# RMS norm sums by VectorE 32x32 turns and a folding matmul in place of TensorE transposes

## The chip, the cores and the metric

One core of a Trainium2 chip runs the whole program. The metric is the device time of one execution in microseconds (us), as the median of several runs. The engines are TensorE (PE, with its weight loads listed apart as PEld), VectorE (DVE), ScalarE (ACT), GpSimd (POOL) and SyncE (SP, which issues most DMAs). Each takes its own instructions in order.

## The reference

The kernel computes one encoder layer for two sequences (prompt and sample, each 512 tokens of width 1024) in fp32. What the change touches are its norms:

```
def rms_norm(x, g):
    xf = x.astype(jnp.float32)
    y = xf * lax.rsqrt(jnp.mean(xf * xf, axis=-1, keepdims=True) + EPS)
    return (y * g.astype(jnp.float32)).astype(x.dtype)
...
    x = x + 0.5 * swiglu(rms_norm(x, ffn1_norm), ffn1_w_gate, ffn1_w_up, ffn1_w_down)
    h = rms_norm(x, mix_norm)
    proj = h @ w_in
...
    att = gqa_block_attention(aq, ak, av)
    mem = mlstm_bidirectional(mq, mk, mv, gate_pre, mlstm_gate_bias, o_pre, mlstm_head_norm)
    merged = jax.nn.sigmoid(g_att) * (att @ w_up_att) + jax.nn.sigmoid(g_mlstm) * (mem @ w_up_mlstm)
    x = x + merged @ w_out
    x = x + 0.5 * swiglu(rms_norm(x, ffn2_norm), ffn2_w_gate, ffn2_w_up, ffn2_w_down)
```

Inside the memory (`mlstm_bidirectional`, four heads of width 128) each head's output has a norm of its own:

```
    h = h * lax.rsqrt(jnp.mean(h * h, axis=-1, keepdims=True) + EPS)
    h = h.reshape(B, S, M_WIDTH) * head_norm.astype(jnp.float32)
    return (jax.nn.sigmoid(o_pre.astype(jnp.float32)) * h).astype(q.dtype)
```

## The kernel before, in words

Activations lie turned: the 128 partitions hold channels, the free axis holds the 512 tokens, so x is eight tiles of 128x512. A norm's mean over channels is then a sum over partitions (and over the eight tiles). Every large product is split into a high and a low part, and three matmuls with 512 columns replace one.

The program runs FFN1 for both sequences, its down projection (`ffn_down`), the mixing stage (`mix`, a generator: `m0` for the prompt, `m1` for the sample), and FFN2 with its end. A scheduler orders the instructions by a running priority; `shifted(n)` moves a stretch's priority later by n. In the attention the PE order is pinned: scores (L1039), gate projections (L776), key transposes (L1055) and values (L1066) stand in program order, and `among` puts a few gate matmuls between them.

A norm goes like this. ACT squares the tiles and an accumulator of 128x512 collects them (`sq_add`, L148 to L156). `col_sums` (L199) transposes the accumulator on PE in four 128x128 pieces (L202), and DVE reduces each piece (L204) to a column: 128x4, one number per token. `rstd_cols` (L158) forms the reciprocal root by an integer guess and three Newton steps on 128x4 (L161 to L191). `bcast_psum` (L208) spreads it again by four PE transposes of broadcast columns (L212), and for x `bcast_cols` copies the result from PSUM into an SBUF tile R (L218). The norms of x stand at four places:

- A: x of m0 at the end of FFN1's down projection (`mid_stats`, L1578);
- B: x of m1, inside the attention of m0 (`mid_parts(1)`, called as `extra` at L1125 after head 2 or 3);
- D: x of m0 before FFN2, inside the attention of m1 (`parts2(0)`);
- F: x of m1 at the start of FFN2 (`stats2(1)`).

The attention part of `mix` scales its projections by R and by the columns r. In the memory part `mem_head` builds a head's weights and `mem_out` (L1218) its output in a PSUM tile: squares (ACT L1238), gates (DVE L1240), norms: `col_sums`, `rstd_cols`, and, with priority moved 160 later, the spread, DVE's scaling of the gated head by its gain and the spread root (L1244, into a row of the tile `box`), and the residual split into `mem` (L1245). While the heads run, PE fills in with matmuls of the attention's merge and of later gates. Behind head 3 come eight gate projections `mem_gate` (L1156): 24 matmuls each into a PSUM tile "mm", which DVE empties into a t2 tile (L1159, times R). Of "mm" banks there are three, of "pst" and "pss" two each, of "pso" one; of the SBUF tiles t2 eleven.

Of the kernel before, what the change touches and what calls it, by code (L numbers as in the profile page):

```python
# [26 lines left out]
def encoder(ctx, tc, I, outs):  # L27
# [44 lines left out]
    def tables(shapes):  # L72

        t = spool.tile([P, 7 * S // 2], F32, tag="tab", bufs=1, name=nm("tab"))
        out, c = [], 0
        for sh in shapes:
            n = sh[0] * (sh[1] if len(sh) > 1 else 1)
            v = t[:, c:c + n]
            out.append(v if len(sh) == 1 else v.rearrange("p (a b) -> p a b", b=sh[1]))
            c += n  # L80
        return out
# [76 lines left out]
    def rstd_cols(v, width, n):  # L158

        a = spool.tile([P, width], F32, tag=f"rs{width}", bufs=5 if width > 2 else 10, name=nm("rs"))  # L160
        nc.vector.tensor_scalar(a, v, 1.0 / n, EPS, op0=ALU.mult, op1=ALU.add)  # L161
        return rsqrt_cols(a, width)
# [29 lines left out]
            y = r  # L192
        return y

    def stats(acc):

        return rstd_cols(col_sums(acc), 4, D)

    def col_sums(acc, bs=(0, 1, 2, 3)):  # L199
        p = PT()  # L200
        for b in bs:
            nc.tensor.transpose(p[:, b * P:(b + 1) * P], acc[:, b * P:(b + 1) * P], ident)  # L202
        c = spool.tile([P, len(bs)], F32, tag=f"cs{len(bs)}", bufs=4, name=nm("cs"))
        nc.vector.tensor_reduce(c, p[:, bs[0] * P:(bs[-1] + 1) * P].rearrange("p (b d) -> p b d", d=P), axis=AX.X,  # L204
                                op=ALU.add)
        return c

    def bcast_psum(r):  # L208

        pr = PT()  # L210
        for b in range(4):
            nc.tensor.transpose(pr[:, b * P:(b + 1) * P], r[:, b:b + 1].to_broadcast([P, P]), ident)  # L212
        return pr

    def bcast_cols(r):
        pr = bcast_psum(r)
        R = T2(F32, "R")
        nc.vector.tensor_copy(R, pr)  # L218
        return R

    def fetch_w(view, behind=None):
# [475 lines left out]

    def mix_consts():
        pin = tc.keep_in_program_order
        tri, msk, *cgs = tables(((4, P), (2, P)) + ((4, DA),) * 4)  # L700
        pin(nc.gpsimd.dma_start(tri, I["c_tri"]))
        pin(nc.gpsimd.dma_start(msk, I["c_mask"]))
        rope = T2(F32, "f2").rearrange("p (c b d) -> p c b d", c=2, b=4)
        pin(nc.gpsimd.dma_start(rope, I["c_rope"].rearrange("c (b p) d -> p c b d", p=P)))
        for name, sc in (("q_norm", DA ** -0.5), ("k_norm", 1.0)):
            gb = cpool.tile([P, DA], F32, name=nm("gb"))
            pin(nc.gpsimd.dma_start(gb, I[name].partition_broadcast(P).rearrange("p a d -> p (a d)")))
            if sc != 1.0:
                G_.tensor_scalar(gb, gb, sc, None, op0=ALU.mult)
            cg, sg = cgs.pop(0), cgs.pop(0)  # L710
            G_.tensor_tensor(cg, rope[:, 0], gb.unsqueeze(1).to_broadcast([P, 4, DA]), op=ALU.mult)
            sgv = sg.rearrange("p b (i two) -> p b i two", two=2)
            srv = rope[:, 1].rearrange("p b (i two) -> p b i two", two=2)
            gbv = gb.rearrange("p (i two) -> p i two", two=2)
            for e in range(2):
                G_.tensor_tensor(sgv[:, :, :, e], srv[:, :, :, e],
                                 gbv[:, :, 1 - e].unsqueeze(1).to_broadcast([P, 4, DA // 2]), op=ALU.mult)
            tabs.append((cg, sg))
        tabs.extend((tri, msk))
# [76 lines left out]
    def mix(s, xh, xl, early=None, extra=None, after=None):  # L796
# [100 lines left out]
        def gates():  # L897
            Gb = Gt.rearrange("p (b c) -> p b c", b=4)
            V_.tensor_tensor(Gb, Gb, gbias.unsqueeze(1).to_broadcast([P, 4, 16]), op=ALU.add)
            Gv = Gt.rearrange("p (b d g h) -> p b d g h", b=4, d=2, g=2)  # L900

            Fs, Fv = gs("Fs")
            Is, Iv = gs("Is")
            for dst, g in ((Fv, 1), (Iv, 0)):
                G_.tensor_copy(dst[:, 0], Gv[:, :, 0, g, :])
                for b in range(4):
                    G_.tensor_copy(dst[:, 1, 3 - b], Gv[:, b, 1, g, :])
            fa, _ = gs("fa")
            V_.scalar_tensor_tensor(fa, Fs, -1.0, Fs, op0=ALU.mult, op1=ALU.min)
            nc.scalar.activation(fa, fa, AF.Exp)  # L910
            nc.scalar.activation(fa, fa, AF.Ln, bias=1.0)
            nc.scalar.activation(warm, fa[:, 0:1], AF.Exp)
            Lt, _ = gs("Lt")
            V_.scalar_tensor_tensor(Lt, Fs, 0.0, fa, op0=ALU.min, op1=ALU.subtract)
            p = PT()
            for d in range(2):
                rhs = Lt[:, d * 16:(d + 1) * 16]
                for j, lhs in enumerate((tabs[2][:, 2 * d, :], tabs[2][:, 2 * d + 1, :], ones)):
                    nc.tensor.matmul(p[:, j * 32 + d * 16:j * 32 + (d + 1) * 16], lhs, rhs, start=True, stop=True)
            V_.tensor_copy(cs, p[:, 0:96])  # L920
            et, ev = gs("et")
            V_.tensor_tensor(et, Is, cs[:, 32:64], op=ALU.add)
            p = PT()
            nc.tensor.transpose(p[0:32, 0:P], et, ident)
            rows = F2()[0:32]
            er, run = rows[:, 0:P], rows[:, P:2 * P]
            V_.tensor_copy(er, p[0:32, 0:P])
            nc.sync.dma_start(ebuf.rearrange("d b h s -> (d b h) s"), er)
            V_.tensor_tensor_scan(run[:, ::-1], er[:, ::-1], er[:, ::-1], NEG, op0=ALU.max, op1=ALU.max)
            V_.tensor_tensor_scan(run[0:16], er[0:16], er[0:16], NEG, op0=ALU.max, op1=ALU.max)  # L930
            top = rows[:, 2 * P:2 * P + 1]
            V_.tensor_reduce(top, er, axis=AX.X, op=ALU.max)
            return run, top
# [241 lines left out]
        def mem_head(h):  # L1175
# [39 lines left out]
                    V_.tensor_scalar(tf[:, up_], tb[:, up_], rb, None, op0=ALU.mult)  # L1215
            return Ts

        def mem_out(h, Ts):  # L1218
            vm = Vm[0]
            po = PO()  # L1220
            hs_ = slice(h * P, (h + 1) * P)
            turned = []
            for j in range(4 + 1):
                if j < 4:
                    p = PT()
                    for i in range(4):
                        nc.tensor.transpose(p[:, i * P:(i + 1) * P], Ts[i][0][:, j * P:(j + 1) * P], ident)
                    ph, pl = T2(F32R), T2(F32R)
                    split(p, ph, pl)
                    turned.append((j, ph, pl))  # L1230
                if j >= 1:
                    t, ph, pl = turned.pop(0)
                    with shifted(15):
                        for n, (a, b) in enumerate(((0, ph), (1, ph), (0, pl))):
                            nc.tensor.matmul(po, vm[:, a, t, hs_], b, start=(t == 0 and n == 0),  # L1235
                                             stop=(t == 3 and n == 2))
            h2 = T2()
            nc.scalar.activation(h2, po, AF.Square)  # L1238
            og = ogs[h]
            V_.scalar_tensor_tensor(og, og, 1.0, po, op0=ALU.add, op1=ALU.mult)  # L1240
            rh = rstd_cols(col_sums(h2), 4, DM)
            with shifted(160):
                Rh = bcast_psum(rh)
                V_.scalar_tensor_tensor(og, og, hn[:, h:h + 1], Rh, op0=ALU.mult, op1=ALU.mult)  # L1244
                split(og, mem[:, h, 0, :], mem[:, h, 1, :])  # L1245

        for h in range(HM):
            Ts = mem_head(h)
            if h == 0:
                go(*mem_values())  # L1250
            queue.append(merge_att(2 * h))
            fill(1)
            mem_out(h, Ts)
            if h + 2 < HM:
                queue.extend([out_gate(h + 2), mem_qk(h + 2, 0), mem_qk(h + 2, 1)])
            queue.append(merge_att(2 * h + 1))
            fill(99)

        mh, ml = A([P, KD, S], F32R, "mh"), A([P, KD, S], F32R, "ml")
# [317 lines left out]

    def mid_stats(s, a=0, b=0):  # L1578
        with shifted(a):
            r[s] = stats(accs[s])  # L1580
        with shifted(b):
            R[s] = bcast_cols(r[s])

    r = [None, None]
    R = [None, None]
# [11 lines left out]
    box()  # L1597

    def mid_parts(s):
        def one():  # L1600
            r[s] = stats(accs[s])

        def two():
            R[s] = bcast_cols(r[s])
        return one, two

    m0 = mix(0, *nhl[0], None, mid_parts(1), prep1)
# [12 lines left out]
        put(xc[B11 if d < HK_ else B21], d % HK_, xt)  # L1620

    def stats2(s):
        r[s] = stats(acc2[s])
        R2[s] = bcast_cols(r[s])

    def parts2(s):
        def one():
            r[s] = stats(acc2[s])

        def two():  # L1630
            R2[s] = bcast_cols(r[s])
        return one, two

    R2 = [None, None]
# [153 lines left out]
```

## Time and profile before

| | |
|---|---|
| time, median of 3 runs | 2062.38 us (2060.41 to 2063.18) |
| profiled execution, span from first to last instruction | 2059.1 us |
| median over that span | 3.3 us |
| granted TensorE clock in it | 0.999 |
| L202 in it (sums) | 52 transposes of 128x128, 32 for heads, 20 for x |
| L212 in it (spreads) | 52 transposes of 128x128, 48 of Newton results |
| L204, reduction of a transposed sum | 13, mean 688 ns |
| narrow Newton operation 128x4 (L188, L189, L191) | 36 each, mean 160 or 161 ns |

A span is shorter than the time of a run, which also holds what lies around the first and the last instruction. In the profile's rows stand the start, the duration, the engine, the line, the operation, output<-input, and in brackets how long the engine stood idle before and which engine's work ended that.

### The profile page before, as it was taken

To read this page: it belongs to the slowest core of one execution; us is meant where nothing else is said; L and a number is where in the kernel's file an instruction comes from. 1 tells how busy PE (TensorE), PEld (TensorE's weight loads), DVE (VectorE), ACT (ScalarE), POOL (GpSimd) and SP (SyncE) were. 2 spreads that over 40 slices of the span, in tenths; PEclk is the share of its full clock that TensorE was granted. 3 is DMA by queue.
4 is the path that set the end of the run, shared out by engine and by line. 5 is a ranking of instruction groups with operands and counts; after the bars stand their busy time and mean duration, and the time that the engine had idled before them with its cause. 6 is when DMAs were issued, how large, how long until landed. Compare 5 with 4: busy or idle time off the path is not lost.

```text
span 2059.1 us, 27038 instructions
## 1 busy us (share of the span) xinstructions
PE 2047.3 (99%) x9445; PEld 1691.3 (82%) x9445; DVE 1553.0 (75%) x2764; ACT 913.0 (44%) x1667; POOL 92.8 (5%) x108
## 2 busy tenths in 40 slices
PE   9999999999999999999999999999999999999998
PEld 7888888888888888888888888888888888888887
DVE  8888889886797787675566756455788888796797
ACT  7544444442235567563334553324544444443224
POOL 0000000001003000100120000001000000000001
PEclk9999999999999999999999999999999999999999
DMA  9656556799766753877684345677656555599753
GB/s 321 198 170 221 177 191 205 243 349 348 260 227 247 223 187 130 278 259 242 197 310 160 109 140 200 196 265 239 202 175 202 194 174 184 186 342 347 276 202 119
DMA packets 311015, 457.97 MB, mean 222 GB/s; under 512 B 20232, under 2 KB 182112, under 8 KB 309600
## 3 DMA queue, kind: packets, MB, share of 16 engines
q1 hardware_dynamic: 308800, 450.27, 64.6%
q0 software_dynamic: 1920, 5.72, 0.9%
q8 instruction: 74, 1.21, 0.2%
q14 instruction: 61, 0.50, 0.1%
q10 hardware_dynamic: 160, 0.27, 0.0%
HBM read 288.25 MB, written 167.94 MB: 222 GB/s over the span
## 4 chain that ended last, share of the span: by engine, by line
PE 97%; DVE 1%; ACT 1%; DMA 1%; issue 0%; SPq 0%; ACTq 0%; DVEq 0%
PE mm L789 15%; PE pso L332 12%; PE pst L332 12%; PE mm L332 10%; PE mm L590 8%; PE pss L332 6%; PE mm L776 6%; PE pst L590 4%; PE pss L590 4%; PE mm L756 4%; PE pso L590 3%; PE pso L1066 1%; PE pss L1039 1%; PE pst L1055 1%; PE pso L1235 1%; PE pss L1185 1%
## 5 line engine op out<-in xcount | busy, mean ns | idle before, releaser
L332 PE MATMUL pst<-xc,w 128*128 128x512 f32 x1056 | 253.6, 389 | 0.0
L332 PEld LDWEIGHTS pst<-xc,w 128*128 128x128 f32 x1056 | 198.3, 188 | 41.1
L332 PE MATMUL mm<-xc,w 128*128 128x512 f32 x972 | 229.9, 390 | 0.2 <-ACT f L340 0.2
L332 PEld LDWEIGHTS mm<-xc,w 128*128 128x128 f32 x972 | 181.9, 188 | 38.1 <-ACT f L340 0.6
L590 PE MATMUL mm<-rt,w 128*128 128x512 f32 x765 | 178.9, 389 | 0.0
L789 PE MATMUL mm<-xh,w 128*128 128x512 f32 x560 | 177.6, 393 | 0.0
L590 PEld LDWEIGHTS mm<-rt,w 128*128 128x128 f32 x765 | 143.6, 188 | 29.8
L290 ACT ACTIVATE w<-t 128x512 fp32r<-128x512 f32 x176 | 106.5, 627 | 135.7 <-issue 63.1
L291 DVE TENSOR_TENSOR w<-t,w 128x512 fp32r<-128x512 f32 x176 | 117.8, 688 | 47.9 <-ACT w L290 46.6
L332 PE MATMUL pss<-xc,w 128*128 128x512 f32 x528 | 126.8, 389 | 0.0
L332 PE MATMUL pso<-xc,w 128*128 128x512 f32 x528 | 126.8, 389 | 0.0
L332 PE MATMUL pso<-xc,f 128*128 128x512 f32 x528 | 126.8, 389 | 0.0
L789 PEld LDWEIGHTS mm<-xh,w 128*128 128x128 f32 x560 | 104.7, 188 | 21.2 <-DVE w L239 0.2
L332 PEld LDWEIGHTS pss<-xc,w 128*128 128x128 f32 x528 | 99.2, 188 | 20.5
L332 PEld LDWEIGHTS pso<-xc,w 128*128 128x128 f32 x528 | 99.1, 188 | 20.5
L332 PEld LDWEIGHTS pso<-xc,f 128*128 128x128 f32 x528 | 99.1, 188 | 20.5
L776 PE MATMUL mm<-xh,w 128*128 128x512 f32 x336 | 114.5, 401 | 0.0
L789 PE MATMUL mm<-xl,w 128*128 128x512 f32 x280 | 109.7, 392 | 0.0
L673 ACT ACTIVATE w<-wr 128x512 fp32r<-128x512 f32 x72 | 45.1, 632 | 137.0 <-PE pso L590 71.4
L673 ACT ACTIVATE w<-t 128x512 fp32r<-128x512 f32 x82 | 51.8, 632 | 107.4 <-PE pst L590 62.4
L590 PE MATMUL pst<-rt,w 128*128 128x512 f32 x396 | 93.7, 389 | 0.0
L590 PE MATMUL pss<-rt,w 128*128 128x512 f32 x396 | 93.7, 389 | 0.0
(407 smaller groups left out, 4037.5 us busy)
## 6 DMA issues: line engine op xcount, KB each, us to landing
rt<-rbuf SPq DMA_DIRECT2D x154, 512.0 KB, 5.7
wpark<-w SPq DMA_DIRECT2D x104, 512.0 KB, 3.4
w<-wpark SPq DMA_DIRECT2D x104, 512.0 KB, 4.8
wr<-in_ffn_w_gate_dram SPq DMA_DIRECT2D x62, 512.0 KB, 5.3
rbuf<-tab SPq DMA_DIRECT2D x102, 256.0 KB, 3.9
wr<-in_ffn_w_up_dram SPq DMA_DIRECT2D x44, 512.0 KB, 4.5
rbuf<-f SPq DMA_DIRECT2D x72, 256.0 KB, 4.1
wr<-in_w_in_dram SPq DMA_DIRECT2D x36, 512.0 KB, 5.7
```

Of the source, the lines that this page charges most:

```text
L290: pin(nc.scalar.activation(t[:, 0], src, AF.Copy))
L291: pin(V_.tensor_tensor(t[:, 1], src, f(t[:, 0]), op=ALU.subtract))
L332: nc.tensor.matmul(p, a[:, k, :], xt[:, b, k, :], start=(first and k == 0 and i == 0), stop=(k == HK_ - 1 and i == 2), skip_group_check=True)
L590: nc.tensor.matmul(p, u[:, a, d * P:(d + 1) * P], r[:, b, ts], start=(first and q == 0 and k == 0), stop=(q == len(us) - 1 and k == 2), sk ...
L673: nc.scalar.activation(hi, src, AF.Copy)
L756: nc.tensor.matmul(p[b][:, :N], a[:, k, bs], w_[:, kl, :], start=(k == 0 and i == 0), stop=(k == KD - 1 and i == 2))
L776: pin(nc.tensor.matmul(p[0], a[:, k, :], b, start=(k == 0 and i == 0), stop=(k == n - 1 and i == 2)))
L789: nc.tensor.matmul(p, a[:, k, :], b, start=(k == 0 and i == 0), stop=(k == n - 1 and i == 2))
L1039: pin(nc.tensor.matmul(p, qT[:, h, b * P:(b + 1) * P], kv[:, hk * 2 + j, :], start=(j == 0), stop=(j == 1)))
L1055: pin(nc.tensor.transpose(p[:, b * P:(b + 1) * P], Ps[b][:, kb * P:(kb + 1) * P], ident))
L1066: pin(nc.tensor.matmul(pos[h], Vst[:, kb, h // 4, :], w, start=(kb == 0 and i == 0), stop=(kb == 3 and i == 1)))
L1185: nc.tensor.matmul(p, qk[a][:, isl], qk[b], start=(n == 0), stop=(n == 2))
```

## The change

`col_sums` and `bcast_psum` are no longer used for the norms of x at mixing and FFN2 and for the heads. In their place:

- `block_sums`: DVE turns the 128x512 tile in blocks of 32x32 (STREAM_TRANSPOSE), so that a block's 32 channels lie along the free axis, and reduces them to 128x16. A partition then holds, for 16 tokens, the sum over 32 of the 128 channels.
- `block_rstd`: one matmul with the constant `fold`, which adds the four partitions that belong together and gives each the total; then the same Newton steps on 128x16 (or 128x64).
- `spread_rows`: a second DVE turn, of the root broadcast 32 times, gives the 128x512 tile that the PE transposes gave.
- `row_cols`: where the columns r are wanted too (A and B), four copies on POOL.
- For the heads, `mem_out` only leaves its 128x16 sums in `hsum`, a t2 tile that lives through the four heads. After head 3, `mem_norm` does the fold, the Newton steps and the spreads for all four at once, without the former shift of 160.

PE loses 96 transposes and gains six fold matmuls. `finish0` at the end of FFN2 and the start of the program keep their transposes.

```
+    def fold_const():
+        part_ = fold[:, 0:32]
+        for a in range(1, 4):
+            src = ident[:, 0:32] if a == 1 else part_
+            nc.gpsimd.tensor_tensor(part_, src, ident[:, a * 32:(a + 1) * 32], op=ALU.add)
+        nc.gpsimd.tensor_copy(fold[:, 32:P].rearrange("p (a j) -> p a j", j=32),
+                              part_.unsqueeze(1).to_broadcast([P, 3, 32]))
+
+    def block_sums(t, to):
+        q = T2()
+        nc.vector.transpose(q, t)
+        nc.vector.tensor_reduce(to, q.rearrange("p (n j) -> p n j", j=32), axis=AX.X, op=ALU.add)
+
+    def block_rstd(v, n, row):
...
+        p = PT()
+        nc.tensor.matmul(p[:, 0:w], fold, v, start=True, stop=True)
...
+        V.tensor_scalar(a, p[:, 0:w], 1.0 / n, EPS, op0=ALU.mult, op1=ALU.add)
...
+    def row_stats(acc):
+
+        row = T2()
+        block_sums(acc, row[:, 0:16])
+        return block_rstd(row[:, 0:16], D, row)
...
+    def row_cols(r16):
+
+        c = spool.tile([P, 4], F32, tag="rc4", bufs=2, name=nm("rc"))
+        for a in range(4):
+            ps_ = slice(a * 32, (a + 1) * 32)
+            nc.gpsimd.tensor_copy(c[ps_, :], r16[ps_, :].rearrange("p (b a) -> p a b", a=4)[:, a, :])
+        return c
+
+    def spread_rows(r16, R):
+
+        nc.vector.transpose(R.rearrange("p (n j) -> p n j", j=32), r16.unsqueeze(2).to_broadcast([P, 16, 32]))
         return R
...
+        hsum = T2()
+
         def mem_out(h, Ts):
...
-            rh = rstd_cols(col_sums(h2), 4, DM)
-            with shifted(160):
-                Rh = bcast_psum(rh)
+            block_sums(h2, hsum[:, h * 16:(h + 1) * 16])
+
+        def mem_norm():
+            rh = block_rstd(hsum[:, 0:64], DM, hsum)
+            for h in range(HM):
+                og = ogs[h]
+                Rh = spread_rows(rh[:, h * 16:(h + 1) * 16], T2())
                 V_.scalar_tensor_tensor(og, og, hn[:, h:h + 1], Rh, op0=ALU.mult, op1=ALU.mult)
                 split(og, mem[:, h, 0, :], mem[:, h, 1, :])
...
+            if h == HM - 1:
+                mem_norm()
             fill(99)
...
     def mid_parts(s):
+        got = []
+
         def one():
-            r[s] = stats(accs[s])
+            got.append(row_stats(accs[s]))
 
         def two():
-            R[s] = bcast_cols(r[s])
+            R[s] = spread_rows(got[0], T2(F32, "R"))
+            r[s] = row_cols(got[0])
         return one, two
```

`mid_stats`, `stats2` and `parts2` change in the same way (the last two without `row_cols`). Lines of the new kernel stand some 45 higher in the rows below: scores are L1084, the residual split is L718, the turn L223, its reduction L224, the fold L234, the spread L262, the evacuation of a memory gate L1204.

In the attention of m0 (place B), PE's rows before, from the values to the next score, a name and a number for each tile:

```order
L1066 MATMUL pso_6390<-t_603_6383,kv_5280 128x512
L1066 MATMUL pso_6390<-t_604_6384,kv_5280 128x512
L202 MATMUL pst_6432<-ident,R_5176 128x128 x4
L1039 MATMUL pss_6460<-kv_5280,qT_5283 128x512 x2
L776 MATMUL mm_6416<-xl_4890,w_6309 128x512
```

And in the changed kernel:

```order
L1111 MATMUL pso_6385<-t_595_6378,kv_5275 128x512
L1111 MATMUL pso_6385<-t_596_6379,kv_5275 128x512
L234 MATMUL pst_6431<-t_608_6427,fold 128x16
L1084 MATMUL pss_6445<-kv_5275,qT_5278 128x512 x2
L821 MATMUL mm_6411<-xl_4895,w_6304 128x512
```

The fold stands where the four transposes stood. The transposes read the accumulator R; the fold reads t_608, the row that DVE's reduction fills. DVE's rows before at that place:

```order
L1012 TENSOR_TENSOR box_5279<-box_5279,tab_4209 128x512
L239 TENSOR_TENSOR w_6410<-wr_6408,w_6410 128x1024
L1049 TENSOR_SCALAR t_608_6398<-t_608_6398,asm_6396 128x512
L674 TENSOR_TENSOR t_615_6424<-pst_6418,t_614_6423 128x512
L204 TENSOR_REDUCE cs_6437<-pst_6432 128x4
L1042 TENSOR_REDUCE asm_6463<-pss_6460 128x1
L161 TENSOR_SCALAR rs_6439<-cs_6437 128x4
```

And in the changed kernel:

```order
L1057 TENSOR_TENSOR box_5274<-box_5274,tab_4214 128x512
L283 TENSOR_TENSOR w_6405<-wr_6403,w_6405 128x1024
L1094 TENSOR_SCALAR t_600_6393<-t_600_6393,asm_6391 128x512
L718 TENSOR_TENSOR t_607_6419<-pst_6413,t_606_6418 128x512
L223 STREAM_TRANSPOSE t_609_6428<-R_5171 128x512
L1057 TENSOR_TENSOR box_5274<-box_5274,tab_4214 128x512
L224 TENSOR_REDUCE t_608_6427<-t_609_6428 128x16
L237 TENSOR_SCALAR t_608_6427<-pst_6431 128x16
```

The turn has the place behind the residual split that the reduction had; a box addition stands between it and its reduction, and the first Newton operation L237 reads the fold's PSUM tile.

At the end of m0's heads (place C), DVE's rows before, from the last residual split of the head's turned weights on: gate 0's evacuation (L1159) stands ahead of head 3's gating (L1240) and sums (L204).

```order
L674 TENSOR_TENSOR t_978_8120<-pst_8114,t_977_8119 128x512
L1159 TENSOR_TENSOR t_1003_8239<-mm_8214,R_5156 128x512
L1240 SCALAR_TENSOR_TENSOR box_5279<-box_5279,pso_8080 128x512
L204 TENSOR_REDUCE cs_8137<-pst_8132 128x4
L161 TENSOR_SCALAR rs_8139<-cs_8137 128x4
```

In the changed kernel, from the last Newton operation of `mem_norm` (L243) to the evacuations of gates 0 and 1 (mm_8102, mm_8138):

```order
L243 SCALAR_TENSOR_TENSOR t_755_7040<-t_755_7040 128x64
L262 STREAM_TRANSPOSE t_934_8036<-t_755_7040 128x512
L262 STREAM_TRANSPOSE t_935_8041<-t_755_7040 128x512
L1295 SCALAR_TENSOR_TENSOR box_5274<-box_5274,hn,t_934_8036 128x512
L1295 SCALAR_TENSOR_TENSOR box_5274<-box_5274,hn,t_935_8041 128x512
L262 STREAM_TRANSPOSE t_936_8046<-t_755_7040 128x512
L718 TENSOR_TENSOR mem_7039<-box_5274,mem_7039 128x512 x2
L1295 SCALAR_TENSOR_TENSOR box_5274<-box_5274,hn,t_936_8046 128x512
L262 STREAM_TRANSPOSE t_937_8051<-t_755_7040 128x512
L1204 TENSOR_TENSOR t_949_8127<-mm_8102,R_5146 128x512
L718 TENSOR_TENSOR mem_7039<-box_5274,mem_7039 128x512
L1295 SCALAR_TENSOR_TENSOR box_5274<-box_5274,hn,t_937_8051 128x512
```

PE's rows of the changed kernel around the fold there; mm_8174 is the bank of gate 2, and gate 3 (mm_8210) takes the bank of mm_8102 and begins 23 matmuls after the fold:

```order
L834 MATMUL mm_8138<-xh_4894,w_8096 128x512
L834 MATMUL mm_8174<-xh_4894,w_8132 128x512
L234 MATMUL pst_8022<-t_755_7040,fold 128x64
L834 MATMUL mm_8174<-xl_4895,w_8132 128x512
L834 MATMUL mm_8174<-xh_4894,w_8132 128x512 x2
```

The sums of four heads now pass through one fold, and the evacuation of gate 0 has moved behind the Newton steps and the four spreads.

More of the change, by code (lines that the diff above doesn't have):

```diff
@@ L193, in rsqrt_cols @@
         return y
-    def stats(acc):
-        return rstd_cols(col_sums(acc), 4, D)
     def col_sums(acc, bs=(0, 1, 2, 3)):
@@ L213, in bcast_psum, with t_ @@
         return pr
[L215 to L218, printed above, removed]
+    fold = cpool.tile([P, P], F32, name="fold")
+    def fold_const():
[10 more added lines that the diff above has]
+    def block_rstd(v, n, row):
+        w = v.shape[-1]
+        cuts = iter(range(w, 512, w))
+        def t_(dt=F32):
+            c = next(cuts)
+            return row[:, c:c + w] if dt is F32 else row[:, c:c + w].bitcast(dt)
+        p = PT()
+        nc.tensor.matmul(p[:, 0:w], fold, v, start=True, stop=True)
+        V = nc.vector
+        a, b, y, u = t_(), t_(I32), t_(), t_()
+        V.tensor_scalar(a, p[:, 0:w], 1.0 / n, EPS, op0=ALU.mult, op1=ALU.add)
+        V.tensor_scalar(b, a.bitcast(I32), 1, None, op0=ALU.logical_shift_right)
+        V.tensor_scalar(y.bitcast(I32), b, -1.0, 1597463007.0, op0=ALU.mult, op1=ALU.add)
+        for _ in range(3):
+            V.scalar_tensor_tensor(u, y, -0.5, y, op0=ALU.mult, op1=ALU.mult)
+            V.tensor_tensor(u, u, a, op=ALU.mult)
+            V.scalar_tensor_tensor(y, u, 1.5, y, op0=ALU.add, op1=ALU.mult)
+        return y
+    def row_stats(acc):
[10 more added lines that the diff above has]
+        nc.vector.transpose(R.rearrange("p (n j) -> p n j", j=32), r16.unsqueeze(2).to_broadcast([P, 16, 32]))
         return R
@@ L699, in mix_consts @@
         pin = tc.keep_in_program_order
+        fold_const()
         tri, msk, *cgs = tables(((4, P), (2, P)) + ((4, DA),) * 4)
@@ L920, in gates @@
             V_.tensor_copy(cs, p[:, 0:96])
-            et, ev = gs("et")
+            et, ev = gs("fa")
             V_.tensor_tensor(et, Is, cs[:, 32:64], op=ALU.add)
@@ L1579, in mid_stats @@
         with shifted(a):
-            r[s] = stats(accs[s])
+            r16 = row_stats(accs[s])
         with shifted(b):
-            R[s] = bcast_cols(r[s])
+            R[s] = spread_rows(r16, T2(F32, "R"))
+            r[s] = row_cols(r16)
     r = [None, None]
@@ L1599, in mid_parts @@
     def mid_parts(s):
+        got = []
         def one():
-            r[s] = stats(accs[s])
+            got.append(row_stats(accs[s]))
         def two():
-            R[s] = bcast_cols(r[s])
+            R[s] = spread_rows(got[0], T2(F32, "R"))
+            r[s] = row_cols(got[0])
         return one, two
@@ L1622, in stats2 @@
     def stats2(s):
-        r[s] = stats(acc2[s])
-        R2[s] = bcast_cols(r[s])
+        R2[s] = spread_rows(row_stats(acc2[s]), T2(F32, "R"))
     def parts2(s):
+        got = []
         def one():
-            r[s] = stats(acc2[s])
+            got.append(row_stats(acc2[s]))
         def two():
-            R2[s] = bcast_cols(r[s])
+            R2[s] = spread_rows(got[0], T2(F32, "R"))
         return one, two
```

## The prediction

> **What bounds the kernel now.** I read the page first: the span, the busy times, and the chain of work that ended last, shared out by engine.
>
> ```profile
> span 2059.1 us, 27038 instructions
> PE 2047.3 (99%) x9445; PEld 1691.3 (82%) x9445; DVE 1553.0 (75%) x2764; ACT 913.0 (44%) x1667; POOL 92.8 (5%) x108
> PE 97%; DVE 1%; ACT 1%; DMA 1%; issue 0%; SPq 0%; ACTq 0%; DVEq 0%
> ```
>
> PE is busy for 2047.3 of 2059.1 us and holds 97% of the chain. An instruction taken off PE therefore shortens the span by PE's step for it, and a wait put into PE's stream lengthens it by its full length. DVE at 75% can take more work on the whole, yet each engine works in order, so a DVE operation that PE waits for pays for everything that stands ahead of it. Of POOL's 92.8 us nothing binds.
>
> The unit of PE is a step, the distance from one matmul to the next; a record's duration is longer, since matmuls overlap. A piece of the chain, then PE's timeline at the first memory head of m0:
>
> ```profile
> 436.51 6.12 PE mm L590 x27
> ```
>
> ```profile
> 842.18 1.07 PE L789 MATMUL mm<-att,w 128*128 128x512 f32 x4
> 843.09 0.60 PE L202 MATMUL pst<-ident,t 128*128 128x128 f32 x4
> 843.44 0.47 PE L789 MATMUL mm<-xh,w 128*128 128x512 f32 x1
> 843.76 0.39 PE L789 MATMUL mm<-xl,w 128*128 128x512 f32 x1
> ```
>
> 27 matmuls in 6.12 us are 0.227 us a step. The last of the four at 842.18 starts three steps later, at 842.86; from there to 843.76 are 0.90 us, and two matmul steps of it are 0.45. **Four transposes cost PE 0.44 us**, 0.11 each.
>
> Do the transposes also wait? The view of line L202 says so for the eight heads:
>
> ```profile
> L202 PE MATMUL pst<-ident,t x32: 271/273/275, 843.1 to 1307.9; 128*128 128x128 f32 x32
>   ACT t L1238: 1.6, 8
> ```
>
> These 0.2 us before each head's first weight load are no loss: the group at 843.09 is one of them, and 0.90 us held nothing but the steps. A weight load may come about 0.2 us late without PE's stream breaking. I subtract 0.15 us of that from every new wait below.
>
> **The change, part by part.**
>
> *Off PE.* Eight heads lose 8 transposes each: 64 × 0.11 = **-7.0 us**. The four norms of x lose 8 each, 0.87 us a norm. What is added is six folding matmuls, plain fp32 with a narrow right side. The nearest row is L919, also fp32, 128x16, whose twelve matmuls stand as 24 records:
>
> ```profile
> 681.12 0.37 PE L919 MATMUL pst<-Lt,ones 128*128 128x16 f32 x2
> 681.35 0.60 PE L919 MATMUL pst<-Lt,tab 128*128 128x16 f32 x4
> 681.79 0.37 PE L919 MATMUL pst<-Lt,ones 128*128 128x16 f32 x2
> ```
>
> Six records from 681.12 to 681.79 are 0.11 us each, two to a matmul: a fold costs 0.22 us. For 128x64 I take the same; a transpose, 128 wide, gives 0.22 too.
>
> *The unknown price: a DVE turn.* No STREAM_TRANSPOSE is in this trace. Its nearest rows read and write the same 128x512 fp32:
>
> ```profile
> L1049 DVE TENSOR_SCALAR t<-t,asm 128x512 f32<-128x512 f32 x49 | 23.9, 487 | 1.5
> L204 DVE TENSOR_REDUCE cs<-pst 128x4 f32<-128x512 f32 x13 | 8.9, 688 | 1.3 <-PE pst L202 1.1
> L239 DVE TENSOR_TENSOR w<-wr,w 128x1024 fp32r<-128x1024 f32 x52 | 65.9, 1267 | 18.0 <-ACT w L238 16.9 <-DMA wpark<-w 0.5 <-DMA wr<-in_w_in_dram 0.4
> ```
>
> At best it is the lean L1049, 0.49 us; at worst it takes two passes, as much as the double-sized L239, 1.27. I take 0.69, the row of most 128x512 operations on DVE, and the same for the spread, which writes 512 elements a partition. The turned sum's reduction costs 0.69, like L204 that it replaces.
>
> [...]
>
> *Norm A (after FFN1, m0).* The first use of R is far behind the fold and DVE is ahead of PE there; I price no wait: -0.87 + 0.22 = **-0.65**.
>
> *Norm B (x of m1, inside m0's attention).* PE's order is pinned, so the fold takes exactly the place of L202, between values and the next score.
>
> ```profile
> 755.52 1.23 DVE L239 TENSOR_TENSOR w<-wr,w 128x1024 fp32r<-128x1024 f32 x1
> 755.59 0.60 PE L202 MATMUL pst<-ident,R 128*128 128x128 f32 x4
> 756.67 0.48 DVE L1049 TENSOR_SCALAR t<-t,asm 128x512 f32<-128x512 f32 x1
> 757.06 0.68 DVE L674 TENSOR_TENSOR t<-pst,t 128x512 fp32r<-128x512 f32 x1
> 757.66 0.68 DVE L204 TENSOR_REDUCE cs<-pst 128x4 f32<-128x512 f32 x1
> 757.80 0.42 PEld L1055 LDWEIGHTS pst<-ident,t 128*128 128x128 f32 x4 [0.43 <-DVE t L674]
> ```
>
> Before, L202 ran at 755.59 and DVE only followed: its reduction came at 757.66, behind a weight split of 1.23 us. Now PE waits for DVE's answer. The same split, normalisation and residual split end at 757.74; the turn takes the slot of L204 at 757.66 and ends at 758.35, one box addition follows to 758.95, the reduction ends at about 759.6. PE's weight load was due at 755.35: 4.25, less 0.15, is **4.1 us of new wait**, with scores, gate matmuls and key transposes queued behind the fold. From it go 0.87 for the transposes and 0.28 of the 0.43 us wait at 757.80, which falls into it; 0.22 comes on: **+3.2**. The twelve Newton operations and the spread behind it I cost at nothing: PE has the score, gate matmuls and key transposes that were already turned. Without that cover they are 2.4 + 0.7 us more.
>
> *Norm D (m0's norm before FFN2, in m1's attention).*
>
> ```profile
> 1134.38 0.69 DVE L674 TENSOR_TENSOR t<-pst,t 128x512 fp32r<-128x512 f32 x1
> 1134.48 0.60 PE L202 MATMUL pst<-ident,R 128*128 128x128 f32 x4
> 1135.12 0.69 DVE L204 TENSOR_REDUCE cs<-pst 128x4 f32<-128x512 f32 x1
> ```
>
> The same place, with a shorter queue: the turn follows the residual split, 1135.0 to 1135.7, the reduction ends at 1136.4. PE's load was due at 1134.25: 2.2 less 0.15. 2.05 - 0.87 + 0.22 = **+1.4**.
>
> *Norm F (m1, start of FFN2).*
>
> ```profile
> 1416.60 0.69 DVE L155 TENSOR_TENSOR R<-R,t 128x512 f32<-128x512 f32 x1
> 1417.34 0.42 PEld L202 LDWEIGHTS pst<-ident,R 128*128 128x128 f32 x4 [0.26 <-DVE R L155]
> 1418.04 0.69 DVE L204 TENSOR_REDUCE cs<-pst 128x4 f32<-128x512 f32 x1 [0.75 <-PE pst L202]
> 1421.16 0.65 PE L212 MATMUL pst<-ident,rs 128*128 128x128 f32 x4 [0.18 <-DVE rs L191]
> ```
>
> Here L202 and L212 waited for DVE, 0.26 and, by its weight load, 0.60 us, about 0.45 of it real. Turn and reduction now end at 1417.3 + 0.7 + 0.7 = 1418.7; the fold stands 20 matmuls after 1414.16, at 1418.7. No wait: -0.87 - 0.45 + 0.22 = **-1.1**.
>
> *Heads, end of m0 (C).* The fold itself comes 12 matmuls, 2.7 us, after the last values; Square, gating, turn and reduction need about as much: +0.2. The price lies behind it. On DVE the whole `mem_norm`, with a weight split inside, now stands **ahead of the evacuation of gate 0** (L1204, shown in the order), and gate 3 needs gate 0's bank of the three. Terms, from the groups of the 128x64 and 128x512 kind, and the evacuation of before in the timeline:
>
> ```profile
> L899 DVE TENSOR_TENSOR gt<-gt,gbias 128x64 f32<-128x64 f32 x2 | 0.5, 225 | 0.1
> L1244 DVE SCALAR_TENSOR_TENSOR box<-box,hn,pst 128x512 f32<-128x512 f32 x8 | 5.9, 743 | 2.9 <-PE pst L212 2.9
> ```
>
> ```profile
> 927.64 0.68 DVE L1159 TENSOR_TENSOR t<-mm,R 128x512 f32<-128x512 f32 x1
> ```
>
> DVE starts about 0.5 us after the fold (PE's tail, as 0.70 from 1417.34 to 1418.04 shows for four transposes). Twelve narrow operations at 0.26 (0.225 and a gap) are 3.1, the split 1.15, four turns, three scalar_tensor_tensor and two residual splits at 0.65 are 5.9, the evacuation 0.7: ready 11.4 us after the fold. PE has 23 matmuls before gate 3, 5.2 us, and the fold's 0.22: **a new wait of 5.9 - 0.15, say +5.6**. Before, the same evacuation ran at 927.64, ahead of the head's norm, and nothing waited.
>
> *End of m1 (E).* The same burst, but 52 matmuls (11.8 us) lie between the fold and the gate that needs the bank, and no weight split stands in it: +0.2 for the fold alone.
>
> *Other.* Eight POOL copies, a constant in FFN1 and one t2 buffer of eleven held through the heads: nothing, covered by POOL's idle 95% and by DVE's work per head, which falls by some 3 us. If the missing buffer bites, it is 1 us or so.
>
> **Sum:** -7.0 - 0.65 + 3.2 + 1.4 - 1.1 + 0.2 + 5.6 + 0.2 = **+1.8 us** on 2059.1. The median of the runs lies 3.3 us above that span; I carry this over: 2062.4 + 1.8 = **2064.2 us**. Bounds of the turn: it enters nine times (once at B, D, E, F, five times at C). At 0.49 the sum is 0.0, at 1.27 it is +7.0.
>
> **The rivals.**
> 1. *The bank wait at C isn't there*, because evacuations get ahead or the mem burst is shorter than its rows. For it: DVE idles before L1159 in the trace of before; against it: the order is fixed, and in-order DVE can't overtake. +1.8 - 5.6 = -3.8: 2058.6 us.
> 2. *All three waits are hidden* (B, D, C): what is left is the PE saving, 10.5 - 1.3, and the old waits of B and F, 0.7: -9.9, 2052.5 us. Against it stand the same fixed orders.
> 3. *The turn is dear*, 1.27 us: the waits at B, D, C grow, +7.0: 2069.4 us. It passes 0.2% from a turn of about 0.95 us on.
> 4. *The chain behind the fold at B bites*: values of the next head wait for residual splits that stand behind the Newton steps and the spread. The price is up to 3.1 us: 2067.3 us; it decides once the cover of about 5 us of PE work is shorter than DVE's queue.
>
> **How the numbers follow.** A measurement of this kernel tells about 0.2%, 4.1 us, from no change. Forecast, with small errors in its terms: 0.38. Rival 1: 0.14, at -3.8 us about half of it beyond 0.2%. Rival 2: 0.16. Rival 3: 0.18. Rival 4: 0.14. Faster is half of rival 1 and rival 2, 0.23; slower rivals 3 and 4, 0.32; within 0.2% the rest, 0.45. The range takes in the edge of rival 2 and the dear turn: 2052 to 2070.
>
> **What would show it.** A STREAM_TRANSPOSE of 0.69 us; PE waiting before the score (L1084) behind the fold, 4 us at B and 2 at D, released by DVE's reduction L224; PE waiting some 5.6 us in m0's gates, released by L1204; and L202 down to 4 transposes, those of the end. Wrong are steps B and D if DVE's queue ahead of the turn is shorter than before's, and C if gate 3 starts without a pause.

## The result and the profile after

The changed kernel takes **2071.26 us** (median of 5 runs, 2069.89 to 2072.20) against 2062.21 us for the kernel before on the same chip (5 runs, 2060.39 to 2063.18): a ratio of **1.0047, 95% interval 1.0035 to 1.0060**. It is slower by some 9 us, where +1.8 us, within 0.2%, was forecast, and 1.3 us above the upper end of the range.

The page of the changed kernel, the lines that answer to those of before:

```profile
span 2067.9 us, 26830 instructions
PE 2044.2 (99%) x9361; PEld 1687.4 (82%) x9361; DVE 1560.2 (75%) x2712; ACT 913.6 (44%) x1667; POOL 96.2 (5%) x120
PE 94%; DVE 2%; DMA 2%; ACT 1%; issue 0%; SPq 0%; DVEq 0%; ACTq 0%
```

PE has 84 instructions fewer, but its busy time fell by only 3.1 us, while the span grew by 8.8. So there are two things to find: time in which PE waits, and work of PE that takes longer than it did. PE's share of the chain fell from 97% to 94%.

The groups of DVE's turns and of PE's folds, and the group of gate matmuls with its wait:

```profile
L223 DVE STREAM_TRANSPOSE t<-t 128x512 f32<-128x512 f32 x8 | 5.6, 705 | 0.0
L262 DVE STREAM_TRANSPOSE t<-t 128x512 f32<-128x512 f32 x8 | 5.4, 697 | 0.1
L234 PE MATMUL pst<-t,fold 128*128 128x16 f32 x8 | 1.5, 260 | 5.8 <-DVE t L224 5.8
L834 PE MATMUL mm<-xh,w 128*128 128x512 f32 x560 | 178.1, 394 | 5.2 <-DVE t L1204 5.2
```

A turn takes 0.70 us, as forecast (0.69). The folds of 128x16 stand behind 5.8 us of waiting for DVE's reduction L224, and the gate matmuls behind 5.2 us for L1204, the evacuation of gate 0: the three waits that the forecast named, at its places. The timeline of the changed kernel at B, DVE and PE:

```profile
754.66 1.23 DVE L283 TENSOR_TENSOR w<-wr,w 128x1024 fp32r<-128x1024 f32 x1
...
756.20 0.69 DVE L718 TENSOR_TENSOR t<-pst,t 128x512 fp32r<-128x512 f32 x1
756.80 0.70 DVE L223 STREAM_TRANSPOSE t<-R 128x512 f32<-128x512 f32 x1
757.43 0.65 DVE L1057 TENSOR_TENSOR box<-box,tab 128x512 f32<-128x512 f32 x1
758.00 0.68 DVE L224 TENSOR_REDUCE t<-t 128x16 f32<-128x512 f32 x1
758.73 0.30 PEld L234 LDWEIGHTS pst<-t,fold 128*128 128x128 f32 x2 [4.29 <-DVE t L224]
...
759.75 1.03 PE L821 MATMUL mm<-xh,w 128*128 128x512 f32 x2
760.58 0.63 PE L821 MATMUL mm<-xl,w 128*128 128x512 f32 x1
761.01 0.63 PE L821 MATMUL mm<-xh,w 128*128 128x512 f32 x1
```

The queue ahead of the fold is the forecast's, operation by operation, and so is its length: 4.29 us. At C and D the same view shows the weight load of gate 3 behind L1204 and that of the fold behind L224:

```profile
943.49 0.29 PEld L834 LDWEIGHTS mm<-xh,w 128*128 128x128 f32 x1 [5.60 <-DVE t L1204]
```

```profile
1144.06 0.30 PEld L234 LDWEIGHTS pst<-t,fold 128*128 128x128 f32 x2 [2.35 <-DVE t L224]
```

**The last three lines of the fence on B are what the forecast does not have.** From 760.58 to 761.01 a matmul takes 0.43 us, where the step was 0.227. The view of busy time by stretches, with the granted clock as the third number from the end of each row, around B, C and D:

```profile
755.00:759.00 4.00, 0.27 (x3) 0.28 (x3) 3.67 (x6) 0.63 (x2) 0.00 (x0) 1.00 0.85 296
760.00:763.00 3.00, 3.00 (x10) 2.41 (x10) 2.65 (x11) 1.55 (x4) 0.71 (x4) 0.50 0.02 7
764.00:767.00 3.00, 3.00 (x17) 2.48 (x16) 1.62 (x5) 1.38 (x3) 0.00 (x0) 1.00 0.00 0
938.00:943.00 5.00, 0.31 (x2) 0.00 (x0) 5.00 (x9) 2.73 (x4) 0.00 (x0) 0.77 0.55 204
944.00:947.00 3.00, 3.00 (x8) 2.31 (x7) 3.00 (x6) 2.02 (x4) 0.00 (x0) 0.50 0.00 0
948.00:951.00 3.00, 3.00 (x15) 2.47 (x14) 0.00 (x0) 0.00 (x0) 0.00 (x0) 1.00 0.80 258
1142.00:1144.00 2.00, 0.14 (x1) 0.00 (x0) 1.89 (x3) 0.28 (x1) 0.00 (x0) 1.00 0.85 291
1146.00:1148.00 2.00, 2.00 (x8) 1.67 (x7) 1.25 (x8) 1.01 (x3) 0.00 (x0) 0.50 0.00 0
1150.00:1152.00 2.00, 2.00 (x13) 1.67 (x12) 1.74 (x4) 1.34 (x3) 0.00 (x0) 1.00 0.00 0
```

Three times the same picture: a stretch in which PE has nothing, then one in which PE is fully busy at a clock of 0.50 and does far fewer instructions a microsecond, then 1.00 again. At C the clock falls already inside the wait (0.77 is its mean from 938 to 943 us); the last section sets that beside PE's idle time. Idle time on the wait is one bill; matmuls at half speed behind it are a second one, and in the busy column they look like work.

The two kernels share 9341 matmuls in the same order, apart from some 150 exchanged neighbours. The start of each in the changed kernel, less its start before, gives an account by place (median over 30 matmuls at each border):

| place | forecast, us | measured, us |
|---|---|---|
| start to A | 0 | -0.15 |
| A | -0.65 | -0.7 |
| B, with the spread | +3.2 | +5.27 - 0.46 = +4.8 |
| heads of m0 | -3.5 | -3.45 |
| C | +5.8 | +6.9 |
| between C and D | 0 | +0.2 |
| D, with the spread | +1.4 | +3.53 - 0.44 = +3.1 |
| heads of m1, E | -3.5 + 0.2 | -1.85 |
| F | -1.1 | -0.9 |
| FFN2, 16 to 56 us behind F | 0 | +0.9 |
| sum | +1.8 | +8.8 |

### The profile page after: what moved, and what is told of

Its sections match the earlier page's. It is cut to its first block, busy times and chain, and to the rows that moved or that the text cites. A ratio compares the mean times of both kernels' runs of the same rounds, so it can differ in the third digit from the quotient of the medians.

```text
span 2067.9 us, 26830 instructions
## 1 busy us (share of the span) xinstructions
PE 2044.2 (99%) x9361; PEld 1687.4 (82%) x9361; DVE 1560.2 (75%) x2712; ACT 913.6 (44%) x1667; POOL 96.2 (5%) x120
## 4 chain that ended last, share of the span: by engine, by line
PE 94%; DVE 2%; DMA 2%; ACT 1%; issue 0%; SPq 0%; DVEq 0%; ACTq 0%
PE mm L834 14%; PE pso L376 12%; PE pst L376 12%; PE mm L376 9%; PE mm L634 8%; PE pss L376 6%; PE mm L821 5%; PE pst L634 4%; PE pss L634 4%; PE mm L801 4%; PE pso L634 3%; PE pss L1084 1%; PE pso L1111 1%; PE pst L1100 1%; PE pso L801 1%; PE pst L834 1%
```

## Experiments

The theory: TensorE pays for a wait twice, with its length and with a stretch at half the granted clock behind it. The rival: the waits cost their length alone, and the rest was lost elsewhere. Times below are medians; the kernel before took 2061.9 us beside the first eight.

**Sums earlier (`e1_sums_early`).** At B and D the turn and its reduction are asked for two steps of the attention ahead of the fold.

```
-                if extra and b == 2 and h in (2, 3):
-                    extra[h - 2]()
+                if extra and (h, b) in ((2, 0), (2, 2), (3, 2)):
+                    extra[((2, 0), (2, 2), (3, 2)).index((h, b))]()
...
+        def sums():
+            got.append(T2())
+            block_sums(accs[s], got[0][:, 0:16])
+
         def one():
-            got.append(row_stats(accs[s]))
+            got.append(block_rstd(got[0][:, 0:16], D, got[0]))
```

> Of the changed kernel (2071.3 us), the turn and its reduction at the two norms inside the attentions (B, D) are asked for two steps of the attention earlier; the folding matmul keeps its place on TensorE. Theory 1 (a wait of TensorE costs its length and, behind it, a stretch at half the granted clock): both waits (4.25 and 2.3 us) and both slow stretches (about 1.7 us each) go, -9 to -10 us, so about 2062 us, and the granted clock stays at 1.00 behind both folds. Theory 2 (the waits cost only their length, the rest of the loss is elsewhere): -6.5 us, about 2064.8 us. If the waits weren't what cost the time, 2071 us.

**Norm later (`e2_norm_late`).** `mem_norm` moves behind the first gates in program order.

```
-            if h == HM - 1:
-                mem_norm()
             fill(99)
...
-        go(*[mem_gate(d) for d in range(KD)])
+        go(*[mem_gate(d) for d in range(4)])
+        mem_norm()
+        go(*[mem_gate(d) for d in range(4, KD)])
```

> Of the changed kernel, the common norm of the four heads is moved behind the first gates of the memory, so that VectorE empties the first three gate banks ahead of it. Theory 1: the wait of 5.6 us for the bank and about 2.0 us of half clock behind it go, about 2063.7 us. Theory 2: only the 5.6 us go, about 2065.7 us. If another resource than the bank held TensorE there, no change.

**Both (`e3_both`).** The two diffs together.

> Both moves together. Theory 1: the gains add up, about 2054.5 us, faster than the kernel before (2062.2 us) by some 7.5 us. Theory 2: about 2059 us. If the two gains are the same gain, about 2062 us.

| | median, us | ratio to before, 95% interval |
|---|---|---|
| sums earlier | 2063.68 | 1.0008, 0.9999 to 1.0017 |
| norm later | 2063.36 | 1.0006, 0.9997 to 1.0015 |
| both | 2055.26 | 0.9968, 0.9956 to 0.9980 |

*Norm later* lies 0.3 us from theory 1 and 2.3 us from theory 2. Its interval, some 1.9 us to either side, would hardly tell them apart, but the trace does: by the shared matmuls C falls by 5.6 us up to the first matmul of gate 3 and by another 1.9 us in the 17 us behind it, where no wait stands. Its stretches:

```profile
937.00:943.00 6.00, 6.00 (x29) 5.00 (x28) 3.73 (x12) 1.58 (x2) 0.00 (x0) 1.00 0.88 320
943.00:948.00 5.00, 5.00 (x24) 4.14 (x23) 4.90 (x10) 2.33 (x3) 0.00 (x0) 1.00 0.73 256
```

Where the changed kernel did 2 matmuls in 5 us, PE is now full, at 1.00. *Sums earlier* gained 7.6 us, between the two theories. By the shared matmuls B and D themselves fall by 4.8 and 3.8 us, 8.6 us together, where theory 2 allowed 6.5; the clock is 1.00 behind the fold at B (760 to 764 us), and D's 3.8 us are more than its wait of 2.35. Other places of the profiled execution took some back. At B one wait was not quite gone. The waits of PE's weight loads between 755 and 765 us in that kernel:

```profile
PEld pst L1100 <- DVE t L718: 1.1, 1, 1.1
```

DVE's residual split is late there by 1.1 us. The 1.4 us of turn and reduction now end 5.5 us ahead of it, and DVE has no idle time in between. *Both* adds the gains up and is faster than the kernel before.

**TensorE kept busy (`e4_keep_busy`).** The waits stay; PE gets matmuls to do in them, whose results the fold overwrites.

```
+        if heat:
+            for _ in range(heat[0]):
+                pin(nc.tensor.matmul(p, heat[1][:, 0, 0:P], heat[1][:, 0, :], start=True, stop=True))
         nc.tensor.matmul(p[:, 0:w], fold, v, start=True, stop=True)
...
-            got.append(row_stats(accs[s]))
+            got.append(row_stats(accs[s], (18, nhl[0][0])))
...
-            got.append(row_stats(acc2[s]))
+            got.append(row_stats(acc2[s], (10, nhl[1][0])))
```

> The changed kernel with its waits left in place, but ahead of the folds at B and D TensorE gets 18 and 10 matmuls that compute nothing that is used (128x512, into the bank that the fold then writes), 4.1 and 2.3 us of them, so that it works while it would wait. Theory 1 (the half clock comes from idleness): the granted clock stays at 1.00 behind both folds, -3.4 us, about 2067.9 us, though the waits are not shorter. Theory 2 (the slow stretch has another cause, or isn't a cost): no gain, 2071.3 us or a little more.

Measured: 2069.61 us. The timeline of this kernel at B, and the stretches behind the fold at B and at D:

```profile
755.58 4.27 PE L236 MATMUL pst<-xh 128*128 128x512 f32 x18
759.68 0.31 PE L237 MATMUL pst<-t,fold 128*128 128x16 f32 x2
759.84 0.70 PE L1087 MATMUL pss<-kv,qT 128*128 128x512 f32 x2
```

```profile
760.00:763.00 3.00, 3.00 (x16) 2.48 (x17) 2.66 (x15) 1.59 (x4) 0.00 (x0) 1.00 0.36 131
1146.00:1148.00 2.00, 2.00 (x10) 1.63 (x9) 1.97 (x9) 0.60 (x1) 0.00 (x0) 1.00 0.04 8
```

The fold is no earlier, and yet the clock is 1.00 in both stretches, where the changed kernel had 0.50, and by the shared matmuls B falls by 1.60 us and D by 1.52. These are the clock's share of the two waits by itself: half the speed over some 3.4 us. It is the trace that shows them. The median fell by 1.6 us, less than its five runs spread (2065.64 to 2071.74); in the profiled execution the program's start, the place at 1296 us and the one in FFN2, below, gave 0.8, 0.7 and 1.3 us back.

**Half as many (`e7_half_busy`).** The same with 9 and 5 matmuls.

```
-            got.append(row_stats(accs[s], (18, nhl[0][0])))
+            got.append(row_stats(accs[s], (9, nhl[0][0])))
...
-            got.append(row_stats(acc2[s], (10, nhl[1][0])))
+            got.append(row_stats(acc2[s], (5, nhl[1][0])))
```

> As the run that kept TensorE busy, with half the idle matmuls: 9 at B, which leaves about 2.2 us without work, and 5 at D, which leaves about 1.2 us. If the clock falls only once a wait is longer than some length between 1.3 us (a wait that did nothing) and 2.3 us (D's wait, which did), D keeps 1.00 behind its fold and gains about 1.5 us locally, and B is at the edge. If any wait of more than 1 us lowers the clock, both places stay slow.

One run, 2068.77 us. The two folds in the timeline, with PE's idle time in brackets, and the stretches behind them:

```profile
759.29 0.40 PE L237 MATMUL pst<-t,fold 128*128 128x16 f32 x2 [1.79 <-DVE t L224]
1144.04 0.40 PE L237 MATMUL pst<-t,fold 128*128 128x16 f32 x2 [0.74 <-DVE t L224]
```

```profile
760.00:763.00 3.00, 3.00 (x12) 2.34 (x10) 2.49 (x13) 0.78 (x2) 0.15 (x1) 0.51 0.21 75
1146.00:1148.00 2.00, 2.00 (x12) 1.73 (x11) 1.90 (x10) 1.13 (x3) 0.00 (x0) 1.00 0.00 0
```

0.74 us of idle PE left the clock alone (D gains 1.59 us), 1.79 us brought it to 0.51, as 3.86 us brought it to 0.50 in the changed kernel (B gains nothing). The bill has a step in it, between these two lengths here; the last section sets it beside PE's idle time by intervals.

**B and D undone (`e5_undo_bd`).** Transposes again at these two norms; heads, A and F as changed. (Two small tags get one buffer instead of two, for room.)

```
         def one():
-            got.append(row_stats(accs[s]))
+            r[s] = stats(accs[s])
 
         def two():
-            R[s] = spread_rows(got[0], T2(F32, "R"))
-            r[s] = row_cols(got[0])
+            R[s] = bcast_cols(r[s])
```

> The changed kernel with the two norms inside the attentions (B, D) turned back to TensorE transposes; heads, A and F as changed. Measured along the stream of common matmuls, B and D cost the changed kernel 4.8 and 3.1 us against the kernel before, wait, slow clock and saved transposes together: about 2063.4 us (theory 1, the clock is part of it); about 2066.7 us if only the forecast's +3.2 and +1.4 us were theirs and the rest came from elsewhere (theory 2).

Measured: 2063.58 us, ratio 1.0007 (0.9998 to 1.0015), where 2063.4 was expected by theory 1. B and D cost the changed kernel 7.7 us in all, not the 4.6 us forecast.

**Heads alone (`e8_heads_only`).** This undoing together with the later norm.

> The heads' part of the change, well placed (common norm behind the first gates), with transposes at B and D again and A and F as changed. Additive: 2063.4 us for B and D undone less 7.9 us for the later norm, about 2055.5 us, so within 1 us of the version with both moves (2055.3 us), because that one still waits 1.0 us at B. If the early turns at B and D are worth their saved transposes, this run is 1.3 to 1.8 us slower than it.

Measured: 2055.99 us, ratio 0.9972 (0.9962 to 0.9982), against 2055.26 for the version with early turns at B and D. The gain over the kernel before comes from the heads, their norm in its new place, A and F; at B and D the turns, even asked for two steps earlier, are worth 0.7 us, inside the two intervals.

**The loads of x2 (`e6_x2_other_queue`).** In the account the heads of m1 miss 1.45 us. The changed kernel's timeline there (SPq is SyncE's queue):

```profile
1291.03 2.82 SPq L1676 DMA_DIRECT2D xnbuf<-f  x2
...
1293.95 0.39 SPq L1674 DMA_DIRECT2D f<-x2buf  x1
...
1299.56 0.75 DVE L713 SCALAR_TENSOR_TENSOR f<-f,gain,R 128x512 f32<-128x512 f32 x1 [2.41 <-DMA f<-x2buf]
...
1302.98 0.53 PEld L1230 LDWEIGHTS pss<-qk,qk 128*128 128x128 f32 x3 [1.34 <-DVE t L1246]
```

Before, all four loads stood ahead of the stores to xnbuf; now the fourth stands behind two of them, each of which waits for a DVE result. DVE then waits for that load with PE's scores queued behind it.

```
-        nc.sync.dma_start(xt, x2buf[0][:, d, :])
+        nc.gpsimd.dma_start(xt, x2buf[0][:, d, :])
```

> The changed kernel, with the eight loads of x2 that prepare FFN2 inside m1's heads issued by GpSimd instead of SyncE. Theory: the fourth load stands on SyncE behind two stores that wait for VectorE, so VectorE sits 2.4 us in front of it and TensorE 1.3 us behind VectorE; on another queue the load comes in time, and the heads of m1 lose 0.9 to 1.2 us, about 2070.2 us in all. Rival: VectorE's load or the t2 buffer held by the sums is the cause, and that stretch stays as it is.

Measured: 2070.29 us, ratio 1.0041 (1.0029 to 1.0054). By the shared matmuls about 1.3 us go at just that place, and DVE's wait for the load is gone. The trace shows the cause; the medians, 1.0 us apart with overlapping intervals, would not. With B and D undone the loads keep the changed order, so it came with the heads.

**Earlier yet (`e9_earlier_yet`).** Both moves, the turns at (1, 0) instead of (2, 0), and the loads on GpSimd's queue.

```
-                if extra and (h, b) in ((2, 0), (2, 2), (3, 2)):
+                if extra and (h, b) in ((1, 0), (2, 2), (3, 2)):
```

> Both moves, with the turn and reduction of B and D a whole head earlier again, and the x2 loads on GpSimd's queue. In the version with both moves TensorE still waits 1.0 us for VectorE's residual split at B, where the kernel before waits 0.3. If it is the turn and its reduction (1.4 us of VectorE) just ahead that are late there, 0.6 us go: about 2054.6 us, and the wait at B falls to 0.3 us. If VectorE is short of time over that whole stretch, the wait stays and the time is 2055.3 us. The loads should bring nothing here, since that version already lost the wait in m1's heads.

Measured: 2053.00 us, ratio **0.9963 (0.9949 to 0.9976)** to the kernel before, which took 2060.87 beside it: the lowest ratio of all, though its interval overlaps that of *both* (0.9956 to 0.9980). The wait at B fell from 1.1 to 0.3 us, and the place gained 0.8 us; a second wait, 0.7 us at about 779 us behind DVE's L1123, went too and gave 0.5 us. DVE was not short of time over the stretch, only at that point. Over m1's heads, where the loads stand, it gained another 0.3 us, where nothing was expected.

## Why the prediction was wrong

Its mechanisms held, but one main term was missing and a small one was set to nothing. By its own steps:

- **The price of a transpose and of a fold** held: the heads of m0 gave 3.45 us of 3.5, A 0.7 of 0.65. The trace's 0.11 us step for a transpose was the right one here.
- **The turn at 0.69 us** held (0.70). The rival of the dear turn, 1.27 us, is out.
- **The waits at B, D and C** held: 4.29, 2.35 and 5.60 us against 4.25, 2.2 and 5.9 before the allowance. Reading DVE's queue ahead of the fold in the new order, priced from the trace of before, gave all three. (At C it wrote 5.6 for 5.9 - 0.15, which is 5.75; that this slip brought the term nearer to the measured wait is luck.)
- **The step that failed** is the sentence on which all three were priced: "a wait put into PE's stream lengthens it by its full length". It costs more. Behind each of the three waits PE works at half the granted clock for 3.4 to 4 us, which cost 1.60 us at B and 1.52 at D (kept busy) and 1.9 at C (norm later): **5.0 us of the 7.0 us by which the sum fell short**. The trace of before had no such wait and a mean granted clock of 0.999; the forecast carried no term for it, in the sum or as a rival.
- **"Other: nothing"** failed in part: the shift of the x2 loads cost about 1.3 us in m1's heads (shown by moving them).
- **F** held where it was looked for (-0.9 of -1.1), but 0.9 us came back in FFN2, where PE waits for ACT's evacuation of a bank (0.44 us at 1462.20 us), which stands behind ACT's weight cast, which waits for a weight load (2.06 us). The other versions lost between 0.3 and 2.2 us there in their profiles, and the one with B and D undone 4 us: there PE stood idle for 1.92 us, and the 21 matmuls behind that took 6.65 us, where 26 took 6.05 us at that place in the changed kernel. At 0.23 us each they would have taken 4.9, so the second bill, by this estimate 1.7 us, came on top. How much of it is the gain given back and how much the chance of one execution stays open; no run took that load out of the way.
- Rival 4, DVE's Newton steps and spread behind the fold at B, didn't occur. At B the wait of 4.29 - 0.15, the clock's 1.60 and the fold's 0.22, less the sums' transposes, 0.44, and the old wait, 0.28, make 5.2 us of the 5.27 measured ahead of the spread; nothing is left to explain.

## What to carry to other kernels

When a sum that the bounding engine waits for moves to another engine, the place of the answer can be worth more than the saved instructions: ask for it early enough that its whole queue has passed, and look how much work covers a burst that stands ahead of an evacuation that frees a bank (here 23 matmuls were too few at C, 52 enough at E). The waits of TensorE that left 1.91 us or more of one of the 3.41 us intervals below idle cost 1.52 us (D), 1.60 (B) and 1.9 (C) of half clock on top of their length: price such a wait with both. Where it can't be removed, matmuls put into it took the second part away here, at B and at D. Read the granted clock behind each new wait, since PE's busy share hides it.

## What the runs showed of the hardware

**In these traces the granted clock changed on a grid.** In the changed kernel it fell at 759.76, 940.66 and 1145.46 us and rose at 763.17, 947.49 and 1148.88 us. The distances between neighbours are 1, 52, 2, 58 and 1 times 3.413 us. The place of the grid differs from run to run: in the half busy kernel the fall at B came at 760.05 us. The falls went with PE's idle time within one interval of it. The stretches cut along the grid at B, in the changed kernel, in the one with x2 loads on GpSimd's queue, and in the half busy one; the first number behind the comma is PE's busy time, the third from the end the clock:

```profile
752.93:756.34 3.41, 1.94 (x11) 1.28 (x9) 3.41 (x7) 2.70 (x5) 0.00 (x0) 1.00 0.43 156
756.34:759.76 3.42, 1.03 (x6) 0.91 (x7) 2.86 (x7) 0.00 (x0) 0.00 (x0) 1.00 0.97 328
759.76:763.17 3.41, 3.41 (x12) 2.72 (x11) 2.83 (x12) 1.72 (x4) 0.73 (x4) 0.50 0.07 28
```

```profile
753.22:756.64 3.42, 1.71 (x10) 1.14 (x8) 3.42 (x7) 2.47 (x5) 0.00 (x0) 1.00 0.68 183
756.64:760.05 3.41, 1.27 (x7) 1.10 (x8) 2.79 (x9) 0.00 (x0) 0.00 (x0) 1.00 0.96 297
```

```profile
756.64:760.05 3.41, 1.62 (x8) 1.08 (x7) 2.89 (x7) 0.00 (x0) 0.00 (x0) 1.00 0.98 327
760.05:763.46 3.41, 3.41 (x11) 2.72 (x10) 2.44 (x13) 0.92 (x3) 0.53 (x3) 0.50 0.17 60
```

An interval at full clock with 1.71 us idle left the next one at 1.00, one with 1.79 us idle brought it to 0.50. In the changed kernel the intervals ahead of the three falls had 2.4 us (B), 2.4 (C) and 1.91 (D) idle, and no other interval at full clock ahead of the end of the program had more than 1.47. In the kernel before the clock fell only at the end, at 2056.22 us, behind an interval in which PE did nothing; no other had more than 0.80 us idle. So in these rows the step lies between 1.71 and 1.79 us, near half the interval. At C the interval at half clock from 940.66 to 944.08 us, with 2.8 us idle, was followed by another at half clock, and that one, in which PE was busy throughout, by one at 1.00, as at B and D.

So where the fall came went with where a wait lay in the grid. At D PE was idle from 1142.14 to 1144.05 us and the clock fell at 1145.46, when PE had been at work again for over a microsecond; at C PE was idle from 938.31 to 943.49 us, the clock fell inside the wait, and the matmuls right behind it were slow. Matmuls of 128x512 whose results nobody reads kept the clock at 1.00 where they left little idle time: 18 at B and 10 at D, with PE busy for all of 755 to 759 and of 1142 to 1144 us, and 5 at D, with 0.74 us idle; 9 at B, with 1.79 us idle, did not.
